# Delta rule: the context tiles' preparations and inverses placed beside the value projections

## Chip, cores and metric

One core of a Trainium2 chip runs the whole program in one launch. The metric is the device time in microseconds (us), and lower is better. Five engines run their own instruction streams in order: TensorE (PE, with its weight loads, PEld), VectorE (DVE), ScalarE (ACT), GpSimd (POOL) and SyncE (SP), which here only issues transfers. ACT issues transfers too, between its own instructions.

## The reference, cut to what matters

The program is a trunk of several transformer blocks over 512 latent tokens and 256 context tokens, in fp32. The first block projects its input to attention heads, to the queries, keys and values of a gated delta rule, and to gates; it runs window attention and the delta rule, merges the two, and ends with an MLP. The delta rule, with chunks of 64 tokens, 8 heads and two directions:

```
kk    = einsum('bhnid,bhnjd->bhnij', kc, kc)
t_mat = eye(CHUNK) + bc[..., None] * dec_strict * kk
w_mat = triangular_solve(t_mat, (bc * eG)[..., None] * kc, lower, unit_diagonal)
u_v   = triangular_solve(t_mat, bc[..., None] * vc,        lower, unit_diagonal)
def step(S, xs):                        # scan over the chunks
    u = uv_c - einsum('bhck,bhkv->bhcv', w_c, S)
    o = einsum('bhck,bhkv->bhcv', qd_c, S) + einsum('bhij,bhjv->bhiv', intra_c, u)
    S = exp(gl_c)[..., None, None] * S + einsum('bhck,bhcv->bhkv', kt_c, u)
    return S, o
o_dc, s_cf, s_cb = bidir_delta(context q, k, v, gates, s_zero, s_zero)
o_dl, _, _       = bidir_delta(latent q, k, v, gates, s_cf, s_cb)
```

What stands before the scan (`kk`, the matrix, its inverse) depends on keys and gates only, not on values, and for each chunk alone. Only the latent outputs are used in the result; of the context the two final states are.

## The kernel before

The 768 tokens are six tiles of 128: tiles 0 and 1 are context, 2 to 5 latent. A dense product in fp32 is three matmuls of split halves (L447, "dense steps" below), 128x512 or 128x256 each, with the weights loaded to `wst`, rounded to `whi` on ACT (L435) and the remainder `wlo` made on DVE or POOL (L108). The stages of the first block that the change touches come in this order:

- **Keys and gates** (`dense_fm`, `delta_gates`): keys for all tiles are convolved, normalised, turned to token-major by PE transposes (L632) and stored by ACT's queue to a DRAM tensor `tok_k` (L648); the gates' running sums go to a DRAM tensor `grows` (L851).
- **Value stage**: the value projections (`conv("v")`, stored to `tok_v`) and the attention queries `aq`. Nothing is woven beside them.
- **Attention** (`window_attention`): first its keys and queries are prepared (norms, rotary tables `Cq`, `Sq`, `Ck`, `Sk`; loads L1229 to L1232), then scores, softmax and products. Beside it run 28 units of `rest`, a generator of 24 dense tiles in 72 units of 8 matmuls, which make the delta queries and the gates `szd`, `sga`, `sgd`.
- **Preparations** (`prep`, `subst`): for each tile in the order 0, 1, 2, 5, 3, 4 the decay differences `Gb`, scale rows `bb` and keys `ktok` are loaded on SP's queue, the keys are transposed on PE (L912), `kk` is made (L928), and DVE writes the scaled matrix into `M[g]` (L935, L938). Step s of the recurrence takes one tile of either direction; group g holds steps 2g and 2g+1, so group 0 is the two context tiles. `subst(0)` then inverts the 32x32 diagonal blocks of group 0 by 31 pairs of DVE instructions (L967, L969), between preparations 1 and 2. Beside all this run 38 more units of `rest`.
- **Merges**: `merges(g)` turns the block inverses into the full 64x64 inverses `O[g]` by small matmuls (L993, L1003, L1006), ACT copies and DVE copies (L1015). `merges(0)` runs with the last 6 units of `rest`.
- **Recurrence** (`chains(g, O[g])`, called `both(g)`): for each step it loads keys and values (L1027, L1028), scales them on DVE (L1030), makes the transposed weights `WT` (L1046), the products `u` (L1059, L1072), and the state update (L1092, L1100, L1102). `subst(1)` and `merges(1)` run beside `both(0)`, `subst(2)` and `merges(2)` beside `both(1)`, and nothing of that kind beside `both(2)`. Beside all three run the output half of attention (`attn_half`) and the modulation vectors (`ada`, L201, with loads `wada` on SP).

`weave` and `side_by_side` take one step from each generator in proportion to the given counts, and so set the order in which instructions are written; a scheduler with a timeline of its own then sets each engine's order, which is fixed in the program. PE never skips an instruction that waits. `psum(True)` takes one of two banks named `mm1`; a pool with one buffer lets a second tile of the same name start only when the first is released.

## Time and profile before

| | us |
|---|---|
| median of 3 runs (lowest to highest) | 2657.61 (2656.32 to 2659.2) |
| the profiled execution | 2662.77 |
| its span in the trace, and what lies around it | 2661.0, 1.8 |
| PE busy in the span | 2473.2 (93%) |
| DVE, ACT, POOL busy | 1488.6, 1004.3, 869.3 |

The profiled execution is 5.2 us longer than the median. The span runs from the first to the last instruction; a stage is read by a window of the trace, which lists the busy time of each engine, the mean clock granted to PE (1.00 is 2.4 GHz, 0.50 is 1.2 GHz) and the share of time in which the transfer engines were busy. Value stage 124 to 186.6, attention 186.6 to 360.7, preparations 360.7 to 450.8, recurrence 450.8 to 665.3.

### The profile page before, as it was taken

The page shows a single profiled execution, that of the slowest core. Times are in us where ns is not written, and L with a number is a line of the kernel's source. Part 1 is how long each engine was busy: PE and PEld are TensorE (multiplying, and loading weights), DVE is VectorE, ACT ScalarE, POOL GpSimd, SP SyncE. Part 2 cuts the span into 40 slices and gives each one's busy share as a digit, 9 for nine tenths or more (in the row PEclk, how much of TensorE's full clock was granted, in tenths as well). Part 3 has the DMA queues.
Part 4 walks back from the last instruction along what each step waited for, and adds up shares of the span by engine and source line. Part 5 has one row for each costly group of instructions (what it writes and reads, how often), then busy time and mean ns, then how long its engine had stood idle before and what let it go on. Part 6 is the DMA issues. An engine that isn't in the chain of part 4 may idle for free.

```text
span 2661.0 us, 40142 instructions
## 1 busy us (share of the span) xinstructions
PE 2473.2 (93%) x16082; PEld 2100.3 (79%) x16082; DVE 1488.6 (56%) x2532; ACT 1004.3 (38%) x1824; POOL 869.3 (33%) x719
## 2 busy tenths in 40 slices
PE   5897997878998999999998999999998999999998
PEld 3786776556887778799787888888887987888888
DVE  4557658875479942252684887666227357522225
ACT  4545453432442222342674512121224365522332
POOL 2443101000742322455324513232235523533331
PEclk8998998789999999999999999999999999999999
DMA  7231164664535533211012244433222101223231
GB/s 258 73 101 44 56 191 152 225 214 162 177 101 183 172 119 95 95 58 37 9 52 92 88 151 126 127 123 119 64 64 63 48 17 62 86 95 98 97 107 48
DMA packets 249144, 282.53 MB, mean 106 GB/s; under 512 B 12167, under 2 KB 207358, under 8 KB 248702
## 3 DMA queue, kind: packets, MB, share of 16 engines
q1 hardware_dynamic: 225582, 249.86, 29.7%
q10 hardware_dynamic: 23376, 30.11, 3.4%
q8 instruction: 126, 2.06, 0.3%
q14 instruction: 60, 0.49, 0.1%
HBM read 264.06 MB, written 15.88 MB: 105 GB/s over the span
## 4 chain that ended last, share of the span: by engine, by line
PE 71%; DVE 15%; DMA 6%; ACT 4%; issue 3%; POOL 1%; SPq 0%; ACTq 0%; POOLq 0%; DVEq 0%
PE mm L447 61%; DMA wada<-in_w_ada_dram 3%; DVE aacc L242 2%; DVE nt L313 2%; PE sc L1825 2%; PE mm L1850 1%; DVE wlo L108 1%; PE mm L1859 1%; PE mm L1354 1%; ACT whi L435 1%; PE u L1072 1%; DMA Gb<-grows 1%; ACT nt L319 0%; DVE tmp L967 0%; DVE X L969 0%
## 5 line engine op out<-in xcount | busy, mean ns | idle before, releaser
L108 POOL TENSOR_TENSOR wlo<-wst,whi 128x1024 fp32r<-128x1024 f32 (+2 forms) x141 | 362.1, 2569 | 777.7 <-ACT whi L435 768.7
L435 ACT ACTIVATE whi<-wst 128x1024 fp32r<-128x1024 f32 (+2 forms) x293 | 287.9, 1031 | 639.8 <-PE mm L447 349.2
L447 PE MATMUL mm<-hmxl,whi 128*128 128x512 f32 (+1 forms) x816 | 314.7, 387 | 3.6 <-DVE hmxl L316 2.8
L447 PE MATMUL mm<-hmxh,whi 128*128 128x512 f32 (+1 forms) x816 | 312.1, 388 | 5.8 <-ACT hmxh L315 5.5
L447 PE MATMUL mm<-hmxh,wlo 128*128 128x512 f32 (+1 forms) x816 | 312.4, 385 | 2.9 <-DVE wlo L108 2.9
L447 PE MATMUL mm<-hidxl,whi 128*128 128x512 f32 (+1 forms) x720 | 280.9, 390 | 7.4 <-DVE hidxl L1478 7.4
L447 PE MATMUL mm<-hidxh,wlo 128*128 128x512 f32 (+1 forms) x720 | 280.1, 389 | 3.0 <-DVE wlo L108 3.0
L447 PE MATMUL mm<-hidxh,whi 128*128 128x512 f32 (+1 forms) x720 | 277.6, 389 | 0.0
L108 DVE TENSOR_TENSOR wlo<-wst,whi 128x1024 fp32r<-128x1024 f32 (+1 forms) x152 | 193.6, 1278 | 148.2 <-ACT whi L435 148.0
L242 DVE SCALAR_TENSOR_TENSOR aacc<-wada,silu,aacc 128x512 f32<-128x512 f32 x280 | 245.9, 925 | 28.0 <-DMA wada<-in_w_ada_dram 27.6
L329 DVE SCALAR_TENSOR_TENSOR xres<-mm,mod,xres 128x512 f32<-128x512 f32 (+1 forms) x122 | 85.0, 702 | 236.5 <-PE mm L447 236.2
L1474 POOL TENSOR_TENSOR nsq<-nt 128x512 f32<-128x512 f32 (+1 forms) x134 | 137.0, 1024 | 152.8 <-ACT nt L1473 129.3
L447 PEld LDWEIGHTS mm<-hmxh,whi 128*128 128x128 f32 x816 | 157.3, 195 | 36.9 <-ACT hmxh L315 6.5
L447 PEld LDWEIGHTS mm<-hmxl,whi 128*128 128x128 f32 x816 | 158.0, 194 | 35.2 <-DVE hmxl L316 4.5
L447 PEld LDWEIGHTS mm<-hmxh,wlo 128*128 128x128 f32 x816 | 157.8, 194 | 34.1 <-DVE wlo L108 4.2
L1478 DVE TENSOR_TENSOR hidxl<-nsq,hidxh 128x512 fp32r<-128x512 f32 (+1 forms) x102 | 78.8, 774 | 172.7 <-POOL nsq L1474 171.2
L447 PEld LDWEIGHTS mm<-hidxl,whi 128*128 128x128 f32 x720 | 136.3, 189 | 37.7 <-DVE hidxl L1478 9.8
L447 PEld LDWEIGHTS mm<-hidxh,wlo 128*128 128x128 f32 x720 | 136.4, 189 | 32.1 <-DVE wlo L108 3.9
L447 PEld LDWEIGHTS mm<-hidxh,whi 128*128 128x128 f32 x720 | 136.2, 189 | 28.2
L1473 ACT ACTIVATE nt<-mm 128x512 f32<-128x512 f32 (+1 forms) x134 | 69.5, 520 | 232.4 <-PE mm L447 232.4
L447 PE MATMUL mm<-whi,h2xh 128*128 128x256 f32 x384 | 110.2, 289 | 3.8 <-ACT raw L1608 2.6
L447 PE MATMUL mm<-wlo,h2xh 128*128 128x256 f32 x384 | 109.0, 286 | 0.0
(517 smaller groups left out, 6031.7 us busy)
## 6 DMA issues: line engine op xcount, KB each, us to landing
wst<-in_w_mlp_dram SPq DMA_DIRECT2D x96, 1024.0 KB, 5.5
wada<-in_w_ada_dram SPq DMA_DIRECT2D x160, 256.0 KB, 2.9
wst<-in_w_in_dram SPq DMA_DIRECT2D x35, 1024.0 KB, 5.4
wada<-in_w_ada_dram SPq DMA_DIRECT2D x48, 512.0 KB, 5.3
wst<-in_w_out_dram SPq DMA_DIRECT2D x10, 1024.0 KB, 6.7
wada<-in_w_ada_dram SPq DMA_DIRECT2D x8, 1024.0 KB, 14.3
xacc<-in_w_out_dram SPq DMA_DIRECT2D x16, 256.0 KB, 2.9
Gb<-grows SPq DMA_DIRECT2D x12, 256.0 KB, 4.3
```

The source lines that it names most:

```text
L108: e.tensor_tensor(out, x, hi.bitcast(F32), ALU.subtract)
L242: nc.vector.scalar_tensor_tensor(acc[j], wt, c, acc[j], ALU.mult, ALU.add)
L313: nc.vector.scalar_tensor_tensor(t, x[:, k, :], a(k), self.rb[n], ALU.mult, ALU.mult)
L329: nc.vector.scalar_tensor_tensor(x[:, m, :], ps[:, :T], gate(m, n), x[:, m, :], ALU.mult, ALU.add)
L435: self.nc.scalar.activation(hi[:, :, c0:c1], st[:, :, c0:c1], AF.Copy)
L447: self.nc.tensor.matmul(ps, lhs[a](k), rhs[b](k), start=first and i == 0, stop=last and i == n - 1)
L1072: self.latest = nc.tensor.matmul(U[d][hc, r * P:(r + 1) * P], WT[d][:, r, hc], S0[d][:, r, :], start=False, stop=r == 3)
L1354: nc.tensor.matmul(po[0:64, :], V[a][:, key, g, :], b, start=i == 0 and a == 0 and b is ph, stop=i == len(kb) - 1 and b is pl)
L1473: nc.scalar.activation(t, ps[:, :T], AF.Relu)
L1474: nc.gpsimd.tensor_tensor(s2, t, t, ALU.mult)
L1478: self.latest = nc.vector.tensor_tensor(lo, s2, hi.bitcast(F32), ALU.subtract)
L1825: mm = nc.tensor.matmul(ps[:, c0:c1], QT_[:, w, t * P:(t + 1) * P], KT_[:, c0:c1], start=w == 0, stop=w == 1)
```

## The change

`delta()` is split. `delta_parts` holds `prep`, `subst` and `merges`; `delta_first` runs the preparations of tiles 0 and 1, `subst(0)` and `merges(0)` woven with the value stage, from a pool of its own with one buffer of each tile, and stores the inverse to a DRAM tensor `first` (1 MB, SP's queue). In `delta` the tile `M[0]` is loaded from `first` on ACT's queue and stands for `O[0]`. The units of `rest` beside attention are 36 in place of 28, and 36 in place of 44 are left for the preparations, where `subst(1)` now follows the four latent tiles. Beside `both(0)` run `merges(1)` and `subst(2)`, beside `both(1)` only `merges(2)`.

```diff
-        self.dense_fm(0, 2, [cm, xm], conv("v", 8, evk))
-        self.dense_tm(0, 2, x_st, keep_aq)
+        parts = self.delta_parts(tokd)
+        first = self.T(self.dram, (P, 2048), "first")
+        self.weave((self.seq(self.dense_fm_steps(0, 2, [cm, xm], conv("v", 8, evk)),
+                             self.dense_tm_steps(0, 2, x_st, keep_aq)), 48),
+                   (self.delta_first(parts, self.pool("df", side="right", ctx=kvs), first), 47))
...
-            self.weave((self.take(rest, 28), 28), (self.seq(kv, units), 130))
+            self.weave((self.take(rest, 36), 36), (self.seq(kv, units), 130))
...
-        oacc = self.delta(tokd, (rest, 44), fill, others, szd, yD)
+        oacc = self.delta(tokd, parts, first, (rest, 36), fill, others, szd, yD)
...
+    def delta_first(self, parts, pool, first):
+        prep, subst, merges, _ = parts
+        M = [self.T(pool, [P, 32, CH], "M0")]
+        O = self.T(pool, [P, 32, CH], "Of")
+        for t in range(2):
+            yield from prep(t, pool, pool, M)
+        yield from subst(0, pool, M)
+        yield from merges(0, O, pool, M)
+        self.nc.sync.dma_start(out=first, in_=O.rearrange("p a c -> p (a c)"))
...
-        TILES = (0, 1, 2, 5, 3, 4)
+        TILES = (2, 5, 3, 4, None)
+        M = [self.T(one, [P, 32, CH], f"M{g}") for g in range(3)]
+        nc.scalar.dma_start(out=M[0].rearrange("p a c -> p (a c)"), in_=first)
...
-            self.weave((seq(preps[0], preps[1], subst(0), preps[2], preps[3], preps[4], preps[5]), 66),
-                       (self.take(early[0], 38), 38))
+            self.weave((seq(*preps, subst(1, one, M)), 64), (early[0], early[1]))
...
-        O = [self.T(op, [P, 32, CH], "O0"), M[0], M[1]]
-        self.weave((merges(0, O[0], op), 5), (early[0], early[1] - 38))
+        O = [M[0], self.T(op, [P, 32, CH], "O1"), M[1]]
...
-        nxt = lambda g: (seq(subst(g), merges(g, O[g], op)), 37)
-        self.weave((seq(self.side_by_side((both(0), 16), nxt(1)), self.side_by_side((both(1), 20), nxt(2)),
-                        both(2)), 142), *[(self.behind(x, marks), n) for x, n in late(ch)])
+        self.weave((seq(self.side_by_side((both(0), 16), (seq(merges(1, O[1], op, M), subst(2, one, M)), 37)),
+                        self.side_by_side((both(1), 20), (merges(2, O[2], op, M), 5)), both(2)), 110), *[(self.behind(x, marks), n) for x, n in late(ch)])
```

How the engines' orders change is shown at three places. PE in the value stage, where the keys of the last context tile (`csg_924`) are transposed for their store; the kernel before:

```order
405 L447 MATMUL mm_194_1048<-hch_102,wlo_805 128x256
406 L447 MATMUL mm_194_1048<-hch_102,whi_804 128x256
407 L632 MATMUL mm_185_1020<-ident_63,csg_924 128x128 x2
408 L447 MATMUL mm_194_1048<-hcl_103,whi_804 128x256
409 L447 MATMUL mm_194_1048<-hch_102,wlo_805 128x256
410 L447 MATMUL mm_201_1094<-hch_102,whi_804 128x256
```

and the changed one, in which L906 is the old L912 and `ktok_1065` are the keys of tile 0, read back from `tok_k`:

```order
406 L447 MATMUL mm_195_1052<-hch_102,whi_804 128x256
407 L632 MATMUL mm_185_1020<-ident_63,csg_924 128x128 x2
408 L447 MATMUL mm_195_1052<-hcl_103,whi_804 128x256
409 L447 MATMUL mm_195_1052<-hch_102,wlo_805 128x256
410 L906 MATMUL mm_202_1073<-ident_63,ktok_1065 128x128 x4
411 L447 MATMUL mm_211_1128<-hch_102,whi_804 128x256
```

Four transposes of `ktok` now stand two matmuls behind the last transpose whose result goes into `tok_k`, and ahead of the value projections that follow.

ACT around the start of attention, where L1229 (in the changed kernel L1250) and the rows after it are the loads for its rotary tables; before:

```order
150 L635 ACTIVATE ct_1452<-mm_248_1447 128x512
151 L648 DMA tok_v_449<-ct_1452 128x4x128
152 L658 ACTIVATE aq_437<-mm_250_1456 128x256
153 L1229 DMA sink_1640<-in_attn_sink_dram 128x8
154 L1230 DMA rope_264_1642<-in_rope_dram 128x512
155 L658 ACTIVATE aq_437<-mm_251_1482 128x256
156 L435 ACTIVATE whi_1509<-wst_1508 128x8x128 x2
157 L1232 DMA gq_1643<-in_q_norm_g_dram 128x64
158 L1232 DMA gk_1644<-in_k_norm_g_dram 128x64
```

and in the changed kernel, where `Of` is the inverse of group 0 and `cy_2130` the first dense tile of `rest`:

```order
175 L658 ACTIVATE aq_437<-mm_284_1846 128x256
176 L435 ACTIVATE whi_2005<-wst_2004 128x8x128 x2
177 L1008 ACTIVATE Of_1062<-mm_287_1899 32x8x32 x2
178 L621 ACTIVATE cy_2130<-mm_309_2012,vec_8_83 128x512
179 L1250 DMA sink_1967<-in_attn_sink_dram 128x8
180 L1251 DMA rope_293_1969<-in_rope_dram 128x512
181 L1253 DMA gq_1970<-in_q_norm_g_dram 128x64
182 L1253 DMA gk_1971<-in_k_norm_g_dram 128x64
183 L1257 ACTIVATE mR_1966<-cst_74 128x256
```

The loads stood among the eight copies of `aq`; now they stand behind the last of them, behind the copies of `Of` and behind the first tile of `rest`.

PE at the start of the recurrence, where the first `u` products are L1059 (in the changed kernel L1083); before:

```order
1723 L1003 MATMUL mm_700_4226<-Z_696_4170,Pm_4215 32x32 x2
1724 L1006 MATMUL mm_700_4226<-Pm_4215,Z_696_4170 32x32 x2
1725 L993 MATMUL mm_703_4283<-Z_697_4171,M_582_3282 32x32 x32
1726 L1059 MATMUL u_4528<-vc_725_4425,O_693_4153 64x64
1727 L1059 MATMUL u_4529<-vc_728_4433,O_693_4153 64x64
1728 L1059 MATMUL u_4528<-vc_725_4425,O_693_4153 64x64 x15
```

and in the changed kernel, where L447 is the output half of attention and L201 the modulation vectors:

```order
1762 L447 MATMUL mm_757_4751<-yAh_1955,wlo_4514 128x512
1763 L447 MATMUL mm_757_4751<-yAh_1955,whi_4513 128x512
1764 L1083 MATMUL u_4777<-vc_734_4519,M_618_3689 64x64 x3
1765 L201 MATMUL mm_724_4490<-wada_4493,silu_93_423 32x256 x4
1766 L1083 MATMUL u_4777<-vc_734_4519,M_618_3689 64x64
1767 L201 MATMUL mm_724_4490<-wada_4495,silu_93_423 32x256 x4
```

The first `u` stood behind the small matmuls of `merges(0)` (L993, L1003, L1006); now it stands behind sixteen matmuls for `WT`, four of L201 and ten of L447.

## Rows read from the trace of the kernel before

**Rows 1.** The chain that ended last, from the page: share of the span by engine.

```profile
PE 71%; DVE 15%; DMA 6%; ACT 4%; issue 3%; POOL 1%; SPq 0%; ACTq 0%; POOLq 0%; DVEq 0%
```

**Rows 2.** Windows by stage: us, then busy PE, PEld, DVE, ACT, POOL, clock, DMA share.

```profile
124.00:186.60 62.60, 60.23 (x407) 54.80 (x406) 29.08 (x63) 26.18 (x57) 27.30 (x23) 1.00 0.36 109
186.60:210.00 23.40, 13.89 (x64) 10.83 (x62) 22.49 (x44) 10.93 (x23) 17.60 (x28) 0.79 0.24 75
210.00:360.70 150.70, 137.96 (x772) 109.91 (x773) 98.62 (x213) 79.70 (x163) 27.43 (x24) 0.96 0.20 61
360.70:450.80 90.10, 86.98 (x658) 70.60 (x656) 65.44 (x120) 38.84 (x50) 3.20 (x6) 0.96 0.60 170
450.80:476.50 25.70, 10.51 (x236) 7.43 (x236) 19.21 (x34) 15.18 (x22) 6.65 (x14) 0.67 0.89 297
476.50:548.40 71.90, 57.32 (x982) 39.08 (x983) 61.92 (x146) 27.84 (x50) 1.50 (x3) 0.81 0.58 185
548.40:612.20 63.80, 53.00 (x930) 38.44 (x930) 44.35 (x98) 19.13 (x36) 0.00 (x0) 0.87 0.74 236
612.20:665.30 53.10, 43.43 (x814) 34.96 (x814) 26.62 (x53) 16.98 (x34) 6.52 (x4) 0.93 0.47 156
462.00:490.00 28.00, 23.99 (x440) 17.23 (x442) 22.65 (x49) 14.58 (x24) 2.14 (x4) 0.62 0.58 186
```

**Rows 3.** Timeline of the value stage: start, us, engine, line, operation.

```profile
116.33 0.39 PE L447 MATMUL mm<-hh,wlo 128*128 128x512 f32 x1
...
116.56 0.40 PE L447 MATMUL mm<-hh,whi 128*128 128x512 f32 x1
...
122.84 2.48 POOL L108 TENSOR_TENSOR wlo<-wst,whi 128x1024 fp32r<-128x1024 f32 x1 [2.27 <-ACT whi L435]
...
123.65 0.38 PE L632 MATMUL mm<-ident,csg 128*128 128x128 f32 x2
```

**Rows 4.** Groups by line on POOL, 360 to 500: xcount, busy, mean ns, idle before.

```profile
L982 POOL MEMSET M<- 32x512 f32 x6 | 3.1, 519 | 74.9 <-DVE M L938 74.0 <-PE mm L993 0.8
...
L961 POOL MEMSET X<- 128x1024 f32 x2 | 1.9, 957 | 24.2 <-DVE Lw L960 24.2
```

**Rows 5.** DMA issues, 70 to 187: KB each, median us to landing.

```profile
tok_k<-ct ACTq DMA_DIRECT2D x4, 128.0 KB, 1.8
...
sink<-in_attn_sink_dram ACTq DMA_DIRECT2D x1, 4.0 KB, 3.0
```

**Rows 6.** DMA issues, 361 to 451: KB each, median us to landing.

```profile
Gb<-grows SPq DMA_DIRECT2D x8, 256.0 KB, 4.3
...
ktok<-tok_k SPq DMA_DIRECT2D x4, 256.0 KB, 7.7
```

**Rows 7.** Table loads on ACT, whole span, by line.

```profile
L625 ACT ACT_TABLE_LOAD x5 | 6.4, 1283 | 3.5 <-DVE cy L623 3.4
```

**Rows 8.** Timeline around the start of attention, ACT queue.

```profile
170.40 0.49 ACTq L1229 DMA_DIRECT2D sink<-in_attn_sink_dram  x1
```

**Rows 9.** Timeline around the start of attention, DVE.

```profile
176.11 2.20 DVE L1240 TENSOR_TENSOR Cq<-rope,gq 128x256 f32<-128x256 f32 x1 [0.35 <-DMA gq<-in_q_norm_g_dram]
```

**Rows 10.** Waits of PE, 187 to 211: us in total, times, longest.

```profile
PE mm L1279 <- ACT ks L1263: 9.2, 2, 6.8
```

**Rows 11.** Chain of waits, 448 to 500: start, us, what.

```profile
455.97 8.78 DMA wada<-in_w_ada_dram
...
476.46 0.44 PE u L1059 x2
```

**Rows 12.** Waits of all engines, 448 to 500.

```profile
PE mm L201 <- DMA wada<-in_w_ada_dram: 11.3, 1, 11.3
```

**Rows 13.** Waits of PE in the recurrence, 476 to 666.

```profile
PE mm L1046 <- DVE M L1015: 6.5, 1, 6.5
...
PE u L1059 <- DVE M L1015: 2.8, 1, 2.8
```

**Rows 14.** Line 626 on POOL over the whole span: durations min/median/max in ns.

```profile
L626 POOL TENSOR_TENSOR csg<-cy,csg x20: 725/1264/1297, 77.7 to 256.1; 128x512 f32<-128x512 f32 x12, 128x256 f32<-128x256 f32 x8
```

More of the change, by code (lines that the diff above doesn't have):

```diff
@@ L853, in delta_gates, with delta_parts, prep @@
                 nc.scalar.dma_start(out=erows, in_=rt)
-    def delta(self, tokd, early, free, late, szd, yD):
+    def delta_parts(self, tokd):
         nc = self.nc
         ident, dl = self.ident, self.dl
-        ds = ExitStack()
-        self.share(True)
-        self.dvelo = True
-        one = self.pool("d1", 1, ctx=ds)
-        rp = self.pool("d2", 4, ctx=ds)
-        pd = self.pool("psD", 2, PSUM, ctx=ds)
-        TILES = (0, 1, 2, 5, 3, 4)
-        M = [self.T(one, [P, 32, CH], f"M{g}") for g in range(3)]
-        X, rec = {}, {}
+        X, rec, loaded = {}, {}, {}
         half = [slice(CH * c, CH * c + CH) for c in range(2)]
-        def prep(t, pool, pool2, loaded={}):
+        def prep(t, pool, pool2, M, rp=None, nxt=None):
             lat = t >= 2
@@ L900, in prep @@
             Gb, bb, kt, qt, qd = loaded[t]
-            i = TILES.index(t)
-            if i + 1 < 6:
-                fetch(TILES[i + 1])
+            if nxt is not None:
+                fetch(nxt)
             nc.vector.tensor_tensor(Gb, Gb, dl["G"][:, t].unsqueeze(3).to_broadcast([P, 2, 8, CH]), ALU.subtract)
@@ L948, in prep, with subst @@
                 yield
-        def subst(g):
+        def subst(g, one, M):
             Lw = self.T(one, [P, 32, 32], "Lw")
@@ L970, in subst, with merges @@
                 yield
-        def merges(g, O, pool):
+        def merges(g, O, pool, M):
             x, m = X[g], M[g]
@@ L1016, in merges, with delta @@
                 yield
+        return prep, subst, merges, rec
+    def delta_first(self, parts, pool, first):
[7 more added lines that the diff above has]
+        self.nc.sync.dma_start(out=first, in_=O.rearrange("p a c -> p (a c)"))
+    def delta(self, tokd, parts, first, early, free, late, szd, yD):
+        nc = self.nc
+        ident, dl = self.ident, self.dl
+        ds = ExitStack()
+        self.share(True)
+        self.dvelo = True
+        one = self.pool("d1", 1, ctx=ds)
+        rp = self.pool("d2", 4, ctx=ds)
+        pd = self.pool("psD", 2, PSUM, ctx=ds)
+        prep, subst, merges, rec = parts
+        TILES = (2, 5, 3, 4, None)
+        M = [self.T(one, [P, 32, CH], f"M{g}") for g in range(3)]
+        nc.scalar.dma_start(out=M[0].rearrange("p a c -> p (a c)"), in_=first)
+        half = [slice(CH * c, CH * c + CH) for c in range(2)]
         St = {}
@@ L1157, in delta @@
             s2 = self.pool("d4", 2, ctx=c)
-            preps = [prep(t, s1, s2) for t in TILES]
-            self.weave((seq(preps[0], preps[1], subst(0), preps[2], preps[3], preps[4], preps[5]), 66),
-                       (self.take(early[0], 38), 38))
+            preps = [prep(t, s1, s2, M, rp, n) for t, n in zip(TILES, TILES[1:])]
+            self.weave((seq(*preps, subst(1, one, M)), 64), (early[0], early[1]))
         op = self.pool("d6", 1, ctx=ds)
-        O = [self.T(op, [P, 32, CH], "O0"), M[0], M[1]]
-        self.weave((merges(0, O[0], op), 5), (early[0], early[1] - 38))
+        O = [M[0], self.T(op, [P, 32, CH], "O1"), M[1]]
         oacc = free()
```

## The prediction

> **What bounds the kernel now.** I read the chain of waits first: 71% of the span is PE's own work [rows 1]. So an edit counts where PE stands idle or runs at a lower clock. The windows by stage [rows 2] give both:
>
> - Value stage: PE busy 60.2 of 62.6 us at clock 1.00, while DVE is busy only 29.1. There is no hole in PE to win, but there is room on DVE.
> - Start of attention: 13.9 of 23.4 at 0.79. DVE is busy 22.5 of 23.4: it makes the keys and tables, and PE waits 9.2 us for one of its results [rows 10].
> - Attention: 138.0 of 150.7, a hole of 12.7. Preparations: 87.0 of 90.1 at 0.96, so PE bounds them too.
> - Recurrence, in four windows: the start up to the first `u` product takes 25.7 us with 10.5 busy at 0.67; then 71.9, 63.8 and 53.1 us for the three groups of steps, the clock rising from 0.81 to 0.93. DVE is busy 61.9 of 71.9 in the first group, 44.4 of 63.8 in the second and 26.6 of 53.1 in the third. The inversions on DVE fall into the first two, and those are the longer ones.
>
> The change takes work out of the last two stages and puts it into the first. Work on PE that only moves (group 0's transposes, products and merges, 48 dense steps from the preparations to the attention) costs the same at both ends. It drops out of the sum except where it fills a hole. What counts is new holes and closed ones.
>
> **Value stage, a hole is added.** PE's order puts four transposes of tile 0's keys two matmuls behind the transposes of the last context keys, which start at 123.65 [rows 3]. Each link from there is sequential. POOL is in its half of a `wlo` until 122.84 + 2.48 = 125.3 [rows 3]; in its new order a memset of X0 (0.96) and four of `Of` (0.52 each) come next [rows 4], so 128.4. Behind these stands the power that normalises these keys; with the product on DVE I take 1.4 us (an estimate from the size of such memsets), so 129.8. Its store to `tok_k` lands 1.8 later [rows 5], at 131.6. Then `ktok` is loaded on SP, median 7.7 in the preparations [rows 6], where the transfer engines are 0.60 busy; the value stage has 0.36 [rows 2]. I take 3.5, about the 3.0 of the small load [rows 5]. PE gets its keys at about 135, having run dry near 124.1: **+11**. Queued behind the waiting transposes are all value projections, and behind those ACT's convolutions.
>
> Three smaller waits follow because each tile has one buffer. The second `Gb` is loaded only when the first is used up: 4.3 [rows 6], then DVE and ACT work on it, while on ACT the next bank of projections stands behind it. The second `ktok` waits for the first transposes. Against 24 dense steps at 0.23 (116.33 to 116.56 [rows 3]) = 5.5 us of cover I take +4. Sum of the stage **+15**. Bounds: +8 if the store and load meet no traffic and the later waits hide; +26 with 7.7 for the load, and with the clock low after the hole, as at 462 to 490, where 24.0 busy us ran at 0.62 [rows 2] and cost 9. `subst(0)` itself is hidden: its 31 pairs run on DVE while PE does the projections, and 33 us of DVE are free.
>
> Four table loads are added on ACT, since the exponential of `Gb` now alternates with the convolution's sigmoid; the trace has 1.28 us for each [rows 7], 5.1 in all, half of it in the waits above. The Trainium skill ("ScalarE: Activation LUTs", section "What ACT_TABLE_LOAD costs") adds a drain of about 1.38 us to each switch. By that rule, as an estimate, two switches on the path would add 2.8 us to the stage and the forecast; by the row they add nothing more.
>
> **Start of attention, a hole grows.** Before, the loads for the tables were issued at 170.40 [rows 8] and `Cq` began at 176.11 [rows 9], both under the 16 us of `aq` that PE still had to do. The first score came 33.9 us after `Cq`, at 210. In the new order of ACT these loads stand behind the last copy of `Of` and the first dense tile of `rest`. So after the end of the value stage PE has one tile (24 steps, 5.5 us), then the load (3.0 [rows 5]), then the DVE chain of about 31 (33.9 less what needs no table): 39.5 to the first score. PE has three dense tiles to cover it, 72 steps, 16.6 us, where it had two in 23.4. Uncovered: 22.9 against 23.4 − 11.0 = 12.4, so **+11**, with DVE nearly full as before. Bounds: +4 (the chain shrinks to 24, since nothing competes for DVE) and +16.
>
> **Attention and preparations.** 24 more dense steps go into the attention proper, where the hole is 12.7 in 150.7; I credit **−1.5** (0 to −4). The preparations lose 48 steps and two context tiles, at PE's own speed; with 3.1 idle there is nothing else to win or lose, 0 (−2 to +5, if four latent tiles under 249 steps run into their own `Gb` loads). Store and load of `first` cost nothing: both run in attention, where transfers are 0.20 busy [rows 2]; on the path, 1 MB at the 297 GB/s of the recurrence's start would take 3.5 us.
>
> **Recurrence, holes close.** At the start, 25.7 us, PE waits 11.3 for the first `wada` [rows 12], whose load alone takes 8.8 [rows 11]; that chain stays. Then `merges(0)` stood ahead of the first `u` at 476.46 [rows 11]. Now `WT`, four L201 and ten L447 stand there; those ten run at the lower clock, some 5 us. First `u` at 11.3 + 1.5 + 5 = 18: 7.7 earlier, of which 5.8 is moved work, so −2. `M` and `O` of the next groups made PE wait 6.5 and 2.8 [rows 13]; with the merges a group earlier both go, −9.3. In the second group DVE loses the rest of `subst(2)`, 11 of its 44 us: −4. The first keeps its load (half of `subst(1)` and all of `subst(2)`, before all of one and half of the other), and gains −2 by a steadier clock. Sum **−17** (−5 to −36). What is late next: keys and `wada` by DMA, 0.47 to 0.74 busy.
>
> **Sum.** 15 + 11 − 1.5 − 17 = +7.5. The profiled execution took 2662.8, so 2670.3; it stood 5.2 above the median, and on the median the forecast is **2665**, 0.28% slower.
>
> **Rivals.**
>
> *Not slower: the recurrence gains twice as much.* If all three groups run at the third's 53.1, it takes 18 + 159 = 177 in place of 214.5: −37.5, less 5.8 moved, −32. For it: DVE's load is the plain difference between the groups. Against: the first still has as many DVE instructions beside it. With the value stage at +10 and the start at +9: 10 + 9 − 1.5 − 32 = −14.5, so **2643**. It decides once the first group takes under 60 us in place of 72.
>
> *Slower: the recurrence is bound by transfers.* In its windows they are 0.58 and 0.74 busy [rows 2]; a chain that is ready earlier then waits for its keys and `wada` instead. The two waits on `M` go, but half comes back: −5. With 26 upstream less 1.5: +19.5, **2677**; with the load of `ktok` at 7.7, 2681. Against: the third group runs faster with a share of 0.47.
>
> *POOL slows beside the inversion.* The convolution's product on POOL takes at most 1.297 us in all 20 cases [rows 14], with DVE idle or busy, so no row speaks for it; if four of those on PE's path in the value stage doubled, that is +5, **2670**. The Trainium skill ("GPSIMD Engine Reference", section "Key points") says that POOL shares its SBUF interfaces with VectorE and contends with instructions of two SBUF inputs, as L967 and L969 are.
>
> **Numbers.** Forecast 0.42 (2665, own range 2655 to 2674), recurrence twice 0.33 (2625 to 2655), bound by transfers 0.20 (2674 to 2690), POOL 0.05. A difference under 0.2% (5.3 us) can't be told from none here. Slower: 0.24 of the forecast's, all of the third case and most of the last: 0.48. Within 0.2%: 0.18. Faster: 0.34. The range 2634 to 2688 leaves out the ends of the second and third case.
>
> **What would show it.** In the changed kernel's trace: PE waiting about 11 us for `ktok` at 124; the first score some 39 us after the last `Of` copy; no wait on `M` in the recurrence; first `u` 18 us after the last dense step; the first group near 70 us, the second near 54. The forecast is wrong if the wait for `ktok` is under 4 us, or if the recurrence is under 180 us.

## The result, and the profile after

The changed kernel takes 2720.1 us (2718.7 to 2721.5) where the kernel before, in the same comparison, takes 2658.4: a ratio of 1.0218, interval 1.0206 to 1.0231. That is slower, as forecast, but by 2.2% and not 0.3%, and outside the range of 2634 to 2688. The profiled execution has a span of 2719.7 us against 2661.0.

The chain that ended last reads almost as before [rows 1]; it doesn't say where 59 us went:

```profile
PE 71%; DVE 14%; DMA 7%; ACT 4%; issue 3%; POOL 1%; SPq 0%; ACTq 0%; POOLq 0%; DVEq 0%
```

The windows by stage of the changed kernel do. Columns as in [rows 2]; the rows are value stage, start of attention, attention, preparations, start of the recurrence, and its three groups:

```profile
124.00:224.20 100.20, 74.31 (x726) 65.50 (x724) 62.37 (x111) 45.86 (x72) 26.58 (x22) 0.86 0.29 84
224.20:273.30 49.10, 27.60 (x117) 21.65 (x108) 32.64 (x82) 15.86 (x41) 24.80 (x36) 0.69 0.22 71
273.30:432.00 158.70, 141.31 (x788) 113.86 (x786) 101.02 (x209) 82.32 (x165) 26.94 (x22) 0.96 0.20 64
432.00:508.90 76.90, 72.68 (x537) 58.62 (x536) 43.10 (x63) 31.13 (x40) 4.97 (x10) 0.96 0.62 168
508.90:525.80 16.90, 6.01 (x53) 4.02 (x52) 14.96 (x36) 4.95 (x8) 2.08 (x5) 0.60 0.92 306
525.80:611.30 85.50, 63.88 (x914) 41.58 (x915) 66.39 (x147) 30.72 (x52) 1.03 (x2) 0.76 0.64 205
611.30:670.90 59.60, 51.38 (x1054) 38.69 (x1048) 31.30 (x66) 17.43 (x35) 0.00 (x0) 0.89 0.57 187
670.90:731.10 60.20, 38.37 (x699) 29.65 (x697) 26.81 (x53) 15.59 (x29) 6.56 (x4) 0.85 0.59 197
```

Against [rows 2], the value stage grows by 37.6 us (62.6 to 100.2) at a clock of 0.86 instead of 1.00, the start of attention by 25.7, the attention by 8.0. The preparations lose 13.2. The recurrence's start falls from 25.7 to 16.9, but its groups take 85.5, 59.6 and 60.2 instead of 71.9, 63.8 and 53.1 (in sum +16.5). What follows the first block's recurrence is 7.1 us shorter. Together that is +58.7.

Six of the large waits of PE in these stages, from the changed kernel's timeline (start, us, operation, then in brackets the idle time and what ended it):

```profile
137.48 1.08 PE L906 MATMUL mm<-ident,ktok 128*128 128x128 f32 x4 [12.87 <-DMA ktok<-tok_k]
176.77 0.55 PE L447 MATMUL mm<-hch,whi 128*128 128x256 f32 x1 [4.98 <-DVE tmp L961]
241.85 0.99 PE L1300 MATMUL mm<-identR,ks 128*128 128x128 f32 x4 [10.31 <-ACT ks L1284]
552.17 1.92 PE L987 MATMUL mm<-Z,M 32*32 32x32 f32 x64 [8.38 <-DVE Z L978]
562.82 0.31 PE L997 MATMUL mm<-Z,Pm 32*32 32x32 f32 x2 [8.74 <-ACT Pm L991]
731.07 0.80 PE L447 MATMUL mm<-yDh,whi 128*128 128x512 f32 x1 [12.48 <-ACT whi L435]
```

The first is the predicted wait for `ktok` (11 forecast, 12.9 found). The last three stand in the recurrence, where the forecast had waits going away. The last of them, on `whi`, was short in the kernel before:

```profile
665.34 0.79 PE L447 MATMUL mm<-yDh,whi 128*128 128x512 f32 x1 [2.42 <-ACT whi L435]
```

Of [rows 13] nothing is left. The wait of [rows 12] for `wada` falls from 11.3 to 3.4, but a new wait of 7.5 for the scaled keys `kb` (L1054, DVE) stands just ahead of it, so the two together are about as long as the one was.

### The profile page after: what moved, and what is told of

Read it like the earlier page. It is cut to its first block, busy times and chain, and to the rows that moved or that the text cites. A ratio compares the mean times of both kernels' runs of the same rounds, so it can differ in the third digit from the quotient of the medians.

```text
span 2719.7 us, 40166 instructions
## 1 busy us (share of the span) xinstructions
PE 2478.9 (91%) x16082; PEld 2104.1 (77%) x16082; DVE 1500.1 (55%) x2531; ACT 1011.8 (37%) x1828; POOL 870.6 (32%) x720
## 4 chain that ended last, share of the span: by engine, by line
PE 71%; DVE 14%; DMA 7%; ACT 4%; issue 3%; POOL 1%; SPq 0%; ACTq 0%; POOLq 0%; DVEq 0%
PE mm L447 60%; DMA wada<-in_w_ada_dram 3%; DVE aacc L242 2%; DVE nt L313 2%; PE sc L1846 2%; PE mm L1871 1%; DVE wlo L108 1%; PE mm L201 1%; PE mm L1880 1%; DVE X L963 1%; PE mm L1375 1%; DVE tmp L961 1%; PE u L1096 1%; DMA wst<-in_w_in_dram 0%; ACT nt L319 0%
## 5 line engine op out<-in xcount | busy, mean ns | idle before, releaser
L108 POOL TENSOR_TENSOR wlo<-wst,whi 128x1024 fp32r<-128x1024 f32 (+2 forms) x142 | 361.7, 2548 | 817.4 <-ACT whi L435 773.9
L447 PE MATMUL mm<-hmxl,whi 128*128 128x512 f32 (+1 forms) x816 | 314.1, 386 | 3.6 <-DVE hmxl L316 2.9
L447 PE MATMUL mm<-hmxh,whi 128*128 128x512 f32 (+1 forms) x816 | 310.7, 386 | 5.9 <-ACT hmxh L315 5.5
L447 PE MATMUL mm<-hmxh,wlo 128*128 128x512 f32 (+1 forms) x816 | 312.1, 384 | 2.5 <-DVE wlo L108 2.5
L108 DVE TENSOR_TENSOR wlo<-wst,whi 128x1024 fp32r<-128x1024 f32 (+1 forms) x151 | 198.5, 1318 | 161.9 <-ACT whi L435 160.1
L447 PE MATMUL mm<-hidxl,whi 128*128 128x512 f32 (+1 forms) x720 | 280.3, 389 | 7.9 <-DVE hidxl L1499 7.9
L447 PE MATMUL mm<-hidxh,wlo 128*128 128x512 f32 (+1 forms) x720 | 279.8, 389 | 2.3 <-DVE wlo L108 2.3
L447 PE MATMUL mm<-hidxh,whi 128*128 128x512 f32 (+1 forms) x720 | 277.2, 388 | 0.0
L1495 POOL TENSOR_TENSOR nsq<-nt 128x512 f32<-128x512 f32 (+1 forms) x134 | 139.2, 1040 | 150.8 <-ACT nt L1494 126.3
L447 PEld LDWEIGHTS mm<-hmxh,whi 128*128 128x128 f32 x816 | 156.6, 194 | 36.4 <-ACT hmxh L315 6.4
L447 PEld LDWEIGHTS mm<-hmxl,whi 128*128 128x128 f32 x816 | 157.5, 193 | 34.9 <-DVE hmxl L316 4.6
L447 PEld LDWEIGHTS mm<-hmxh,wlo 128*128 128x128 f32 x816 | 157.4, 193 | 33.3 <-DVE wlo L108 3.7
L447 PEld LDWEIGHTS mm<-hidxl,whi 128*128 128x128 f32 x720 | 136.1, 189 | 38.2 <-DVE hidxl L1499 10.6
L447 PEld LDWEIGHTS mm<-hidxh,wlo 128*128 128x128 f32 x720 | 136.0, 189 | 31.2 <-DVE wlo L108 3.2
L447 PEld LDWEIGHTS mm<-hidxh,whi 128*128 128x128 f32 x720 | 135.9, 189 | 27.7
L447 PE MATMUL mm<-whi,h2xh 128*128 128x256 f32 x384 | 110.4, 290 | 3.8 <-ACT raw L1629 2.6
L447 PE MATMUL mm<-hh,whi 128*128 128x512 f32 x256 | 107.1, 418 | 3.7 <-ACT kTd L907 1.9
```

The source lines that it names most:

```text
L108: e.tensor_tensor(out, x, hi.bitcast(F32), ALU.subtract)
L447: self.nc.tensor.matmul(ps, lhs[a](k), rhs[b](k), start=first and i == 0, stop=last and i == n - 1)
L1495: nc.gpsimd.tensor_tensor(s2, t, t, ALU.mult)
```

## The experiments

All are compared with the kernel before, which took 2659.2 to 2664.7 in their five comparisons. To follow where time goes, each profiled execution is cut at five events: the value stage's first transpose (L632, at 115 to 117 us in all), the first score, the last product with V (`attention` ends), the first product with `yD`, and the end. The first column is the median of the run's times; the others are of its profiled execution, which lay up to 7 us from that median. "PE idle" is the part of the time to the first score in which PE was not busy.

| run | us | to first score | PE idle | attention | to first `yD` | rest |
|---|---|---|---|---|---|---|
| before | 2658.4 | 94.5 | 11.9 | 150.8 | 304.5 | 1995.7 |
| changed | 2720.1 | 157.5 | 47.4 | 158.7 | 299.1 | 1988.6 |
| scratch in O[1] | 2713.7 | 156.8 | 46.9 | 158.6 | 282.5 | 1991.7 |
| old order of recurrence | 2704.1 | 155.3 | 47.9 | 161.3 | 285.9 | 1984.8 |
| both of these | 2694.8 | 157.1 | 46.1 | 158.6 | 271.8 | 1988.6 |
| later start | 2715.4 | 153.6 | 47.5 | 160.2 | 294.3 | 1988.9 |
| tables early | 2715.8 | 153.7 | 44.2 | 168.5 | 284.3 | 1989.7 |
| products off POOL | 2719.5 | 156.6 | 45.2 | 163.7 | 296.9 | 1986.4 |
| queries behind | 2721.9 | 155.8 | 41.8 | 160.6 | 297.8 | 1986.3 |
| short substitution | 2708.2 | 144.0 | 37.4 | 158.7 | 298.1 | 1989.6 |
| preparations only | 2683.0 | 130.8 | 31.6 | 161.4 | 283.2 | 1991.1 |
| the same, later | 2686.3 | 121.1 | 24.5 | 158.5 | 296.8 | 1990.0 |
| the same, own memory | 2678.9 | 113.8 | 12.3 | 162.2 | 297.3 | 1987.2 |
| before, keys beside | 2677.3 | 91.5 | 3.5 | 166.7 | 311.0 | 1995.1 |
| before, own memory | 2673.7 | 103.4 | 6.1 | 150.5 | 305.8 | 1990.7 |

Attention and the stretch behind it trade time with each other; their sum is 452.8 to 460.6 in the six runs whose code there is the changed kernel's own. A difference of 4 us in that sum means little. The kernel before differs by 5.5 us between its comparisons, so versions from different comparisons are better compared by their ratios to it. By the intervals of these ratios, the scratch alone, later start, tables early, products off POOL and queries behind can't be told from the changed kernel (1.0206 to 1.0231); the other six with moved work are faster than it.

**Scratch.** The output's scratch was the first inverse's buffer, which is `M[0]` since the change.

```diff
-            sg, sq = (O[0][:, 16 * i + 8 * x: ...
+            sg, sq = (O[1][:, 16 * i + 8 * x: ...
```

> Edit: the output step of the recurrence takes its scratch from the inverse of group 1 instead of that of group 0. Theory A (the weights of the next projection share memory with M[0], which the changed kernel keeps in use to the last output step): the 12.5 us wait of PE ahead of that projection falls to 2 to 4 us, 2720 becomes 2708 to 2712. Rival (that load is late because SP's queue issues it behind other loads or transfers are full): the wait stays at 10 or more, 2717 to 2722.

2713.7 us (ratio 1.0199, interval 1.0179 to 1.0218). The mechanism holds, by the place of a transfer and the length of a wait. In the changed kernel the weights behind the recurrence are loaded only after the last use of the scratch (the `yDl` at 720.07); SyncE's row:

```profile
720.90 1.30 SPq L422 DMA_DIRECT2D wst<-in_w_br_dn_dram  x2
```

and with the scratch elsewhere the same load, and PE's wait:

```profile
694.28 0.93 SPq L422 DMA_DIRECT2D wst<-in_w_br_dn_dram  x2
```

```profile
713.71 0.80 PE L447 MATMUL mm<-yDh,whi 128*128 128x512 f32 x1 [2.85 <-ACT whi L435]
```

The load leaves 19 us before the product that needs it instead of 10, and 12.48 becomes 2.85. The median lies between the two theories, and the profiled execution, with a span of 2705.4, is the fastest of four; so what the wait is worth in time is known only roughly.

**The old order of the recurrence.** Substitutions and inverses 1 and 2 are written as before; the value stage keeps the change.

```diff
-            self.weave((seq(*preps, subst(1, one, M)), 64), (early[0], early[1]))
+            self.weave((seq(*preps), 32), (early[0], early[1]))
...
+        nxt = lambda g: (seq(subst(g, one, M), merges(g, O[g], op, M)), 37)
```

> Edit: inversion and merges of groups 1 and 2 are again woven as before the change (inversion 1, then merges 1 beside the first group, 2 beside the second); the value stage keeps the change. Theory A (in the first group PE waits in order for merges 1, 8.4 us for DVE's inversion and 8.7 behind ACT's copies, with a low clock after both): the first group falls from 85.5 to 64 to 70 us, waits on M of 6 to 10 come back, the recurrence falls from 222 to 205 to 212, 2702 to 2712. Rival (the recurrence is bound by transfers or DVE's load, which this edit raises): 220 to 230, 2718 to 2730.

2704.1 us (1.0154, 1.0132 to 1.0176), as theory A had it; the recurrence takes 211 us instead of 222. The waits on `Z` and `Pm` at 552 and 563 are gone. The waits on `M` that theory A expected back are small (1.6 us the longest). The changed kernel's ACT rows at that place show how the second arises:

```profile
552.15 5.10 ACT L1005 ACTIVATE O<-Z 32x512 f32<-32x512 f32 x8 [3.60 <-DVE Z L978]
557.26 4.25 ACT L953 ACTIVATE X<-M 32x1024 f32<-32x1024 f32 x4
561.53 0.63 ACT L733 ACTIVATE ga<-ga 128x512 f32<-128x512 f32 x1
562.18 1.20 ACT L991 ACTIVATE Pm<-mm 32x512 f32<-32x512 f32 x2
```

`merges(1)` stands ahead of `subst(2)` in one sequence, and ACT's order has the four copies that open `subst(2)` (4.25 us) ahead of the `Pm` that the merge still needs; PE, in order, waits 8.74 us with the recurrence's own products behind it. The wait on `Z` is plainer: `subst(1)` began on DVE at 507, at the end of the preparations, and ends at 550.

**Both.** The two edits above in one kernel.

> Both repairs of the recurrence together: the output's scratch lies in the second group's inverse instead of the first's, and the substitutions and inverses 1 and 2 are woven as in the kernel before. Theory A (the two losses are separate): the wait of 12 us before the first product with yD falls under 4 us, and the time is that of the old weaving alone (2704.1) less the wait, 2688 to 2697 us. Rival B (something else, the clock or the weights behind, takes the place of the wait): 2700 to 2706 us although the wait is gone.

2694.8 us (1.0112, 1.0092 to 1.0131), theory A. From the last product with V to `yD` it takes 271.8 us, 27.3 less than the changed kernel and 32.7 less than before. The losses add up. But of the 32.7 us, 23.5 are busy time of PE, work that has moved to an earlier stage; PE's idle time in this stretch is 44.2 against 53.4, a gain of 9.2 where the forecast had 17, and it comes with the old order of the recurrence, not with the new one.

**Later start.** `delta_first` begins 12 weaving steps later, so that the keys have landed.

```diff
-                   (self.delta_first(...), 47))
+                   (self.seq(iter([None] * 12), self.delta_first(...)), 59))
```

> Edit: the preparations beside the value stage start 12 weave steps later. Theory A (PE waits in order for keys whose store, reload and normalisation had no cover, and runs at a low clock behind that): the 12.9 us wait for ktok falls under 2 us and the value stage from 100 us (124 to 224) to 80 to 85, 2720 becomes 2700 to 2706. Rival (the stage is bound by the chain of preparation, inversion and merge on DVE, 31 pairs and all): the end of the merges does not move or moves out, the stage stays above 95, 2716 to 2725.

2715.4 us (1.0206, 1.0191 to 1.0221), 0.6 under rival B's band, and rival B's mechanism. The wait for `ktok` is gone, and another stands at the end of the stage:

```profile
210.04 3.62 PE L987 MATMUL mm<-Z,M 32*32 32x32 f32 x128 [13.67 <-DVE Z L978]
```

So the largest wait of the value stage is not its price. The substitution ends at 208 us without the wait and at 209 with it, and up to the first score PE idles 47.5 us against 47.4.

**Short substitution.** The first substitution alone is cut: it leaves out 24 of its 31 steps, so its inverse is not the reference's.

```diff
-        yield from subst(0, pool, M)
+        yield from subst(0, pool, M, 7)
```

> The changed kernel with the first substitution cut to 7 of its 31 steps (the inverse of the first group is therefore not the reference's); preparations, transposes, inverse and store stay. Theory A (the serial chain on DVE sets the value stage's end, the wait for the keys doesn't): 33 of the 39 us of substitution go, PE has left 24 us less idle time to lose, first score 128 to 140 us after the stage's first transpose instead of 157.5, 2690 to 2704 us. Rival B (the early waits, the clock behind them and the inverse set it): first score at 150 us or later, 2711 us or more.

2708.2 us (1.0178, 1.0163 to 1.0194); the first score at 144.0 lies between the theories. The part of the chain on DVE that was cut is worth 13.5 of the 63 us by which the first score is late, not most of it: behind it PE is full, and the wait for `ktok` (12.2), the low clock behind that and 22.4 us of waits for `ks` at the start of attention remain. Windows of this run, columns as in [rows 2]:

```profile
135.00:155.00 20.00, 17.71 (x125) 16.23 (x126) 6.31 (x13) 5.45 (x9) 3.84 (x3) 0.81 0.24 68
155.00:175.00 20.00, 17.37 (x101) 14.23 (x100) 9.35 (x14) 13.79 (x18) 6.15 (x5) 0.83 0.33 92
...
195.00:215.00 20.00, 20.00 (x369) 18.12 (x368) 4.15 (x6) 11.75 (x22) 4.54 (x2) 1.00 0.22 68
```

**Preparations only.** Only `prep` of the two context tiles stays beside the values; `M[0]` goes through DRAM, and `subst(0)` and `merges(0)` are made where they were before. The rest of the recurrence is as before too, in its order and its scratch.

```diff
-        yield from subst(0, pool, M)
-        yield from merges(0, O, pool, M)
-        self.nc.sync.dma_start(out=first, in_=O. ...
+        self.nc.sync.dma_start(out=first, in_=M[0]. ...
```

> Only the two preparations stay beside the value projections; their products (M of the first group) are kept in DRAM, and the first substitution and inverse are made where the kernel before makes them, as are the other two. Theory A (the chain preparation, substitution of 39 us on DVE, transposes, inverse is longer than the value stage's own 63 us and so its tail is uncovered): first score 112 to 128 us after the value stage's first transpose instead of 157.5 (before: 94.5), and 2665 to 2682 us. Rival B (the stage loses by the wait for the keys and by the low clock behind it, whatever follows): the first score at 140 us or later and 2692 us or more.

2683.0 us (1.0061, 1.0037 to 1.0085), 1 us above theory A's band, and the first score at 130.8 is 3 us above its own. Against the kernel with both repairs, which also has the substitution and the inverse beside the values, the first score comes 26 us earlier, and the stretch behind the attention is only 11.4 longer (283.2 against 271.8). So moving these two costs 26 us and wins back 11.

**The same, later.** As above, with the preparations begun 4 of now 14 weaving steps later.

> As the run with the preparations alone beside the value projections (2683.0 us, first score 130.8 us after the stage's first transpose), but the preparations begin 4 of then 14 weaving steps later, so that their loads have landed. Theory A (the early waits for the loads and the low clock behind them are what the preparations cost there): the waits of 6.3 and 3.3 us before 140 us go, first score at 116 to 126 us, 2668 to 2678 us. Rival B (the preparations' own work and what they push behind themselves cost it): 127 to 134 us, 2679 to 2688 us.

2686.3 us (1.0103, 1.0083 to 1.0122). The first score comes 9.7 us earlier, as A said, but the time doesn't fall and lies in rival B's band. The stretch to `yD` is 13.6 longer, with two waits in it that the run before did not have:

```profile
546.99 1.92 PE L987 MATMUL mm<-Z,M 32*32 32x32 f32 x64 [4.46 <-DVE Z L978]
...
556.99 0.31 PE L997 MATMUL mm<-Z,Pm 32*32 32x32 f32 x2 [8.09 <-ACT Pm L991]
```

Its code there is the same; its order is not. The scheduler arranges each engine's queue again when an earlier stage moves, and what that gives or takes is as large as the gain.

**Own memory.** As the last, but the attention's tables, keys and values lie in pools opened ahead of the value stage. Its first four loads move there with the pools; the products behind them stay at the same place of the program.

```diff
+        kv = self.early_keys(evc, akv)
         kvs = ExitStack()
```

> The run with the preparations alone, begun later (first score 121.1 us after the value stage's first transpose, 2686.3 us), and the attention's tables, keys and values in memory of their own, written at the same place of the program. Theory A (attention's first instructions stand behind the last use of the memory that the preparations of the delta rule hold; the loads were issued 2 to 5 us behind the store of its result in four runs): with memory of their own the loads and norms start before that store, first score at 98 to 114 us, 2668 to 2680 us. Rival B (the place in the program or the queues of DVE and ACT hold them): loads still behind the store, first score at 118 to 124 us, 2682 to 2690 us.

2678.9 us (1.0061, 1.0046 to 1.0076), theory A. In the changed kernel the attention's first load leaves at 231.58; ACT's queue:

```profile
231.58 0.36 ACTq L1250 DMA_DIRECT2D sink<-in_attn_sink_dram  x1
```

With memory of its own it leaves at

```profile
73.54 0.33 ACTq L1249 DMA_DIRECT2D sink<-in_attn_sink_dram  x1
```

That is not memory alone, since this load was also written earlier. The split of the values is the cleaner sign: it needs none of these loads and was not moved, and on DVE it goes from the first place (the run before) to the second:

```profile
200.59 1.29 DVE L1287 TENSOR_TENSOR Vl<-akv,Vh 128x128 fp32r<-128x128 f32 x6
```

```profile
82.75 0.47 DVE L1285 TENSOR_TENSOR Vl<-akv,Vh 128x128 fp32r<-128x128 f32 x2
```

So the attention's pools wait for memory that the stage ahead still uses. The kernel before has this too (the same split runs there at 179.85, and at 82.24 with own memory), but with work put beside the values the stage ahead ends later. Which last use holds the pools is not shown. For the first load it is not the store of the result, which theory A's sentence names: in the changed kernel that store leaves at 227.70 and lands at 232.37, behind the first load, and with the later start the load leaves at 225.78, the store at 226.89.

The store now comes 17 us later (205.65 against 188.63), and the score follows it by 25.0 us instead of 48.3. The first score is only 7.3 us earlier, since PE also works 5.0 us longer ahead of it. PE's idle time up to it shows the gain better. Windows of the kernel before, of the preparations begun later, and of these with own memory:

```profile
115.40:210.00 94.60, 82.72 (x519) 73.19 (x517) 55.94 (x115) 40.72 (x84) 48.35 (x52) 0.95 0.31 94
```

```profile
115.90:236.90 121.00, 96.47 (x626) 83.97 (x625) 63.53 (x133) 52.84 (x98) 50.88 (x54) 0.89 0.34 102
```

```profile
116.80:230.60 113.80, 101.52 (x631) 87.43 (x632) 56.39 (x96) 51.44 (x88) 47.76 (x40) 0.91 0.34 102
```

The idle time is 11.9, 24.5 and 12.3 us: with own memory, PE waits no longer than in the kernel before, though longer than that kernel would with own memory too (6.1).

**Tables early** and **queries behind.** The rotary tables alone ahead of the value stage; and the query projection behind the inverse instead of beside it (`self.dense_tm(0, 2, x_st, keep_aq)` after the weave).

> Edit: the loads and products for attention's rotary tables are written ahead of the value stage. Theory A (the start of attention grew because these loads stand behind the inverse of group 0): the 49 us from the end of the merges to the first score fall to 40 to 42, 2710 to 2714. Rival (DVE's chain of norms and rotations is what lost its cover, tables or not): 46 or more, 2716 to 2720.

> The query projection of the attention (24 of the 48 steps that lie beside the inverse) comes behind the inverse instead of beside it. Theory A (attention's start is a chain of its own on ACT and DVE that begins when the inverse's last copies are made, and PE's work only fills it): the projection fills PE there, but the value stage waits longer, first score within 6 us of after's 157.5 us from the stage's first transpose, 2713 to 2724 us. Rival B (the projection was the cover of attention's start, and the chain in the value stage is hidden by the values alone): first score 15 to 22 us earlier, 2698 to 2706 us.

2715.8 us (1.0211, 1.0195 to 1.0227) and 2721.9 us (1.0215, 1.0192 to 1.0237); the first score comes 3.8 and 1.7 us earlier. With the tables early, the time lies between the two bands: the score follows the store of the inverse by 41.3 us instead of 45.6, but the substitution ends 4.9 us later. With the queries behind, theory A holds: PE fills the start with them (the wait of 10.3 on `ks` goes), yet the score comes hardly sooner. So neither the tables nor the lost cover decides.

**Products off POOL.** The value convolution's products and, by `dvelo`, all low parts of the weights (L108) go to DVE; memsets and a power of 8 columns (L642) stay on POOL.

```diff
+        self.dvelo = True
...
-                nc.gpsimd.tensor_tensor(sg, y, sg, ALU.mult)
+                (nc.vector if which == "v" else nc.gpsimd).tensor_tensor(sg, y, sg, ALU.mult)
```

> From the start of the value stage to its end nothing with two inputs runs on POOL: the products cy*sigmoid of the value convolution and all low parts of the weights are made on DVE. Theory A (a DVE instruction that starts beside a two-input POOL instruction ends only when that one has ended): no instruction of the substitution in the value stage takes over 0.45 us (after: up to 2.34), its 62 instructions take 21 to 23 us instead of 28.2, and the time is 2714 to 2719 us, less than after's 2720 by no more than 6 since DVE has ten more instructions of 0.7 to 1.2 us. Rival B (the long instructions come from something else, as memory or the semaphores): some stay over 1 us, and the time is 2721 to 2727 us.

2719.5 us (1.0206, 1.0179 to 1.0233). The mechanism of A is shown (last section), its gain isn't: the time that DVE no longer spends waiting goes to the products it has taken over, and the substitution still ends at 209 us.

**The kernel before, with the keys beside the values, and with own memory.**

> The kernel before, without the change; only the attention's preparation of keys and values (six tiles: norm, rotary products, split, transposes) lies beside the value and query projections instead of behind them. Theory A (attention's start is a chain of ACT, POOL and DVE that can be hidden beside the projections: PE is busy 13.9 of the 23.4 us before the first score): first score 78 to 90 us after the value stage's first transpose (before: 94.5), and 4 to 14 us faster than before. Rival B (the chain's instructions hold up the convolutions' in the queues of DVE, POOL and ACT, or the query's preparation is the chain that decides): the first score at 91 to 98 us, the time within 4 us of before's.

> The kernel before, with the attention's tables, keys and values in memory of their own, written at the same place of the program. Theory A (memory decides when attention's start can begin, in this kernel too): loads issued before 160 us instead of 170.4, first score 84 to 91 us after the value stage's first transpose instead of 94.5, and 3 to 9 us faster than before. Rival B (what is won at the first score is given back in the attention, as in the run with the keys beside the projections): first score earlier, the time within 4 us of before's or above.

2677.3 us (1.0045, 1.0030 to 1.0061; a second time 2677.1) and 2673.7 us (1.0047, 1.0031 to 1.0062). Theory A fell in both, and neither rival has both the score and the time right. The first score came 3.0 us earlier in the one, and the attention gave back 15.9; in the other it came 8.9 later. This lateness is no waiting: PE idled less up to the score than before (6.1 us against 11.9), but the order put 503 dense steps ahead of it instead of 454. Why that kernel is slower in the end is not shown. No version beats the kernel before.

## Why the prediction was right in sign and wrong in size

Nearly every term of the forecast was idle time of PE. From the windows, idle is the length less PE's busy time; the last column is how much PE's busy time grew:

| stage | forecast | idle before | idle after | found | busy |
|---|---|---|---|---|---|
| value stage | +15 | 2.4 | 25.9 | +23.5 | +14.1 |
| start of attention | +11 | 9.5 | 21.5 | +12.0 | +13.7 |
| attention | −1.5 | 12.7 | 17.4 | +4.7 | +3.3 |
| preparations | 0 | 3.1 | 4.2 | +1.1 | −14.3 |
| recurrence | −17 | 50.2 | 62.6 | +12.3 | −4.6 |
| sum | +7.5 | | | +53.6 | +12.2 |

With the 7.1 us that are regained behind, this is the +58.7. The sign was right, but the forecast gave "slower" only 0.48, and its two signs of being wrong (a wait for `ktok` under 4 us, a recurrence under 180) did not appear: they did not cover a recurrence that grows.

- **Recurrence, the step that failed: "Sum −17", found +12.3, 29 of the 51 us missed.** The waits on `M` went as forecast, and first `u` came 16.9 us after the last dense step (18 forecast). Idle time fell at the start by 4.3 and in the second group by 2.6, but it grew in the first group by 7.0 and in the third by 12.2; the first was to gain 2 "by a steadier clock", and the third had no term. What is "late next" was sought in transfers. In the third group it was a wait for weights, since the output's scratch had moved with `O[0]` into `M[0]` (10.1 us more than before). In the first it was a queue order in which the second inverse waits on DVE and ACT (8.4 and 8.7 us). Both could be read ahead: I had read PE's order at the start of the recurrence, not ACT's at the merges, nor who else uses `O[0]`. With both undone, PE idles 44.2 us from the last product with V to `yD`, instead of 66.8.
- **Value stage, +15, found +23.5.** The wait for `ktok` was right (11, found 12.9), and the smaller ones behind it were near (4, found 4.9); a wait of 5.0 behind the substitution on DVE (at 176.77) had no term. The sentence that failed is "`subst(0)` itself is hidden ... 33 us of DVE are free". Free time is not room for a serial chain: the substitution takes DVE from 169.95 to 208.92, almost whole (19.2 of 20 us busy from 180 to 200), and transposes and merges follow. Adding up waits counted the holes that show first; the later start only moved them. To the first score, cutting 24 of the 31 steps gives 13.5 us, and landing the loads first, where no chain follows, 9.7.
- **Start of attention, +11, found +12.0: a right number by luck.** The order was right: the loads stood behind the last copy of `Of` and left 7.4 us after the stage's end. But the sum was 39.5 us to the first score with 16.6 busy, and it was 49.1 with 27.6 busy; the two misses cancel. From load to score it took 41.7 us, about the 39.6 of the kernel before, where 34 was forecast. That memory holds up this stage was not seen; it is shown in the kernel with the preparations alone, and was not tried in the changed one. The wait of [rows 10] is on ACT's `ks`, not on a result of DVE.
- **Busy time, forecast to cancel, found +12.2.** The work only moved, but PE ran at a mean granted clock of 0.86, 0.69 and 0.76 in the value stage, the start of attention and the first group, where it had 1.00, 0.79 and 0.81. That the clock makes the whole of the 12.2 us was not tried by itself. The forecast had this as an upper bound of the value stage alone.
- **Attention −1.5, preparations 0:** 6.2 and 1.1 us too low. **The 7.1 us behind `yD`** were not foreseen. Of them, 6.1 are PE's busy time for the same 10708 matmuls (1913.1 against 1919.2 us); no experiment says why.
- **Table loads:** the Trainium skill's drain ("ScalarE: Activation LUTs", section "What ACT_TABLE_LOAD costs") doesn't show; the first of the new switches begins as the instruction before it ends and is followed at once:

```profile
132.27 1.06 ACT L913 ACTIVATE Gb<-Gb 128x1024 f32<-128x1024 f32 x1 [4.18 <-DVE Gb L898]
...
133.34 1.28 ACT L914 ACT_TABLE_LOAD   x1
134.64 1.06 ACT L914 ACTIVATE Gb<-Gb 128x1024 f32<-128x1024 f32 x1
```

- **Rivals.** The recurrence did not gain twice the forecast. Transfers don't bind it: their share in its groups is 0.64, 0.57 and 0.59, two of the three long waits are on DVE and ACT, and the third is for a load that the scratch held back. The case of POOL had the right pair of engines and the wrong victim.

The preparations alone, begun late, lose 26.6 us to the first score (121.1 against 94.5). Of these, 12.6 are idle time, and nearly all of that goes with own memory (about half of which the kernel before gains by it too); the other 14.0 are busy time of PE, in which moved work, clock and order were not separated. It stays open why no version with moved work is faster in the end.

## What to carry to other kernels

Before moving a chain of small instructions beside another stage, write down its length from end to end, and compare it with the stage, not its busy time with the idle time of an engine. Ask of every buffer that changes its place or its name who else uses it and which pool takes its memory next: here the wait for weights came from that, and in the kernel with the preparations alone the late start of attention. Work that is fully hidden where it stands (PE was busy 87 of 90 us there) has nothing to give when it is moved. And measure a stage by the idle time of the engine that bounds it, not by when its first result comes: the order may have put more work ahead of that result.

## What the runs showed of the hardware

A DVE instruction that reads two inputs from SBUF (the on-chip memory of the tiles) and meets a POOL instruction with two inputs ends only when that one has ended. Three such POOL rows in the changed kernel's value stage, and the DVE rows that began beside them:

```profile
191.35 1.29 POOL L626 TENSOR_TENSOR csg<-cy,csg 128x512 f32<-128x512 f32 x1 [5.87 <-issue]
194.88 2.55 POOL L108 TENSOR_TENSOR wlo<-wst,whi 128x1024 fp32r<-128x1024 f32 x1 [2.25 <-ACT whi L435]
201.28 1.50 POOL L626 TENSOR_TENSOR csg<-cy,csg 128x512 f32<-128x512 f32 x1 [3.85 <-ACT csg L625]
```

```profile
191.38 1.53 DVE L961 TENSOR_TENSOR tmp<-Lw,X 128x255 f32<-128x255 f32 x1
195.10 3.42 DVE L108 TENSOR_TENSOR wlo<-wst,whi 128x1024 fp32r<-128x1024 f32 x1
201.67 1.36 DVE L963 TENSOR_TENSOR X<-X,tmp 128x220 f32<-128x220 f32 x1
```

POOL ends at 192.64, 197.43 and 202.78; the DVE instructions, which take 0.4, 1.2 and 0.4 us alone, end 0.25 to 1.1 us later. Of the substitution's other long instructions, the longest ends 0.06 us behind a low part on POOL (174.53 and 174.47). With the products and low parts taken off POOL, the substitution's instructions in the same stretch (count, then ns least, median and most) are

```profile
L963 DVE TENSOR_TENSOR tmp<-Lw,X x31: 192/359/425, 169.8 to 208.6; 128x31 f32<-128x31 f32 x2, 128x60 f32<-128x60 f32 x2, 128x87 f32<-128x87 f32 x2, 128x112 f32<-128x112 f32 x2
L965 DVE TENSOR_TENSOR X<-X,tmp x31: 192/358/426, 171.2 to 208.9; 128x31 f32<-128x31 f32 x2, 128x60 f32<-128x60 f32 x2, 128x87 f32<-128x87 f32 x2, 128x112 f32<-128x112 f32 x2
```

where the longest were 1.53 and 2.34 us, and their sum falls from 28.1 to 21.1. A memset on POOL (0.96 us from 506.99) holds up nothing: the DVE pairs beside it take 0.21 to 0.22. Nor does POOL's power of 8 columns (L642, 149.68 to 151.32): the L898 on DVE that begins beside it at 150.63 takes 1.22 us, as it does alone in the preparations. The Trainium skill ("SBUF — State Buffer", section "SBUF: two separate sides") calls the shared ports an exclusive lock, held for the whole instruction, between a DVE instruction with two SBUF inputs and a POOL instruction that reads SBUF; the three pairs of rows and the memset agree; the power of 8 columns, which has two inputs as well, does not show it.
